# ScalarE casts the second block's weights before the operands of the sums; 13 temporaries in a norm; pools laid out anew

## The chip, the cores and the metric

The kernel runs on one core of one Trainium2 chip. The metric is the device time of one launch in microseconds (us); of the kernel before, three runs are known. One launch was also recorded by the hardware profiler; all rows below come from that record. The core's engines are TensorE (PE, matrix products), VectorE (DVE), ScalarE (ACT), GpSimd (POOL) and SyncE (SP, which here only starts transfers).

## The reference

The reference is a trunk of two layers on 1024 prompt tokens and 64 sample tokens, 1088 columns in all. Each layer has a mixer (layer 0: attention and a gated recurrence; layer 1, "odd": a convolution and a linear recurrence) and a feed-forward part. Cut to what matters here:

```python
for l in range(2):
    hn = rms_norm(x, norm_mix[l]) * (1 + sc1) + sh1
    o = even_mix(hn, ...) if l == 0 else odd_mix(hn, ...)
    x = x + (1 + g1) * o
    hn = rms_norm(x, norm_ffn[l]) * (1 + sc2) + sh2
    x = x + (1 + g2) * ((silu(hn @ wg[l]) * (hn @ wu[l])) @ wd[l])
y = rms_norm(x, final_norm)
```

D_MODEL is 1024, the hidden width of the feed-forward part is 2816. Everything is float32.

## The kernel before, in words

Tokens lie along the free dimension, features along the 128 partitions; x is 8 tiles of 128x1088. Each float32 operand of a product is split into a high part (a cast on ACT, `split`, shown as L99) and a low part (operand minus high part, on POOL or DVE, L100), and each product is three products: high by high, high by low and low by high.

The program runs in stages: mix (layer 0, to about 878 us), up half of layer 0 (to about 1380), down half of layer 0 (`ffn0`, to about 1697; its last part also works out the norm statistics and the first projections of the next mixer), odd (to about 2059), up half of layer 1 (to about 2525), down half of layer 1.

**The up half.** It makes 22 blocks of 128 hidden rows, f = 0 to 21, from weights wg and wu. Block 0 is computed while the normalised input is made (its last matmuls are `ps_z`; L385 is ACT's silu of the gate, L386 DVE's multiplication by the up part, L397 the transfer of the finished hidden block). Block 1 (`plain_block`, matmuls at L381) uses the plain input operands and four half weights: wg and wu give two halves each, each half cast on ACT (`wh`) and subtracted on POOL (`wl`). Blocks 2 to 21 (matmuls at L509, in the changed kernel L507) use a scheme with seven products instead of eight, X, Y, Z, W, X, Z, W, whose operands are sums of quarters of the input. `sums()` makes those operands once per layer: ACT adds the shift into x in place (L472, 16 instructions: a 1024- and a 64-column part of each of 8 tiles), DVE subtracts quarters (L477 to L480, 16 instructions of 128x544), and 16 quarters are split, by a cast on ACT and a subtraction on DVE (L99 and L100, `op`). Each block's weights are combined too: `weights(f)` yields the first half weight as it is fetched (X), and the second (Y) after three additions on DVE (s1, wu, wg: these carry L51).

Two `cbc` tiles are also made in the up half: a sigmoid on ACT (L186) and a product on DVE (L187), for the modulation vectors of later stages; the sigmoid and the silu need different ACT tables, so an ACT_TABLE_LOAD stands wherever they follow each other.

**What sets the order.** Instructions made through `oS`, `oV`, `oPE` (class InOrder, so the line shown is L51) keep the order of the source among themselves; the others are placed by the scheduler from their priorities (`soon()` raises them, `later()` lowers them). Each engine then runs its own list strictly in order and waits at an instruction until what it reads is there. `layout` places the buffers of a stage's pool by tag; a tile waits for the last users of the old tile at its address.

**The norm in ffn0's tail.** The squares of the 8 x tiles (`ntmp`) are summed for one chunk of columns after the other; ACT makes some of the squares (L256, L260; for the last chunk L51), DVE adds them (L261, L263), PE reduces them over the partitions (`ps_o <- ones, ntmp`), POOL takes the power (L234, `r`), and then x is normalised (L273, L279, L276, L277).

**The odd stage** handles one of 8 column groups j after the other: each iteration has two projections whose weights are loaded by `load_x` and `load_g`, a convolution (`xc`), gates (`rg`, `mu`), a scan and a part of the output.

Of the kernel before, what the change touches and what calls it, by code (L numbers as in the profile page):

```python
# [10 lines left out]
F32 = mybir.dt.float32  # L11
# [3 lines left out]
AF = mybir.ActivationFunctionType  # L15
ALU = mybir.AluOpType

P = 128
# [36 lines left out]
def hybrid_encoder(ctx: ExitStack, tc: tile.TileContext, I, O):  # L55
# [369 lines left out]
    def up_half(l, plain, x, t_tag, op_tag, ada):  # L425
        B = B12, B11, B21, B22 = plain[0]
        with phase_pool(f"up{l}") as fp:
            layout(fp, ("t4", NT, 4), ("t1", NT, 4), ("t3", NT, 4), ("pad", 72, 1), ("wg", 1024, 2), ("wu", 1024, 1),
                   ("wh", 512, 5), ("cbc", 1024, 2), ("s1", 512, 1), ("wl", 512, 5), ("hid0", NT, 2))
# [6 lines left out]
            def w_split(src, pair=None):  # L436
                hi, lo = pair or w_pair()
                with soon():
                    split(src, hi, lo, G)
                return hi, lo  # L440
# [26 lines left out]
            def sums():  # L467

                for k in range(KD):
                    for r0, rn, b in rng(0, NT):  # L470
                        v = x[k][:, r0:r0 + rn]
                        S.activation(v, v, AF.Identity, bias=mods[l][:, 3 * KD + k, b:b + 1])  # L472
                T1, T3, T4 = ([halves(fp.tile([P, NT], F32R, name="op", tag=t, bufs=4)) for _ in range(4)]
                              for t in ("t1", "t3", "t4"))
                for k in range(4):
                    a, b, c, d = x[k][:, :HT], x[k][:, HT:], x[k + 4][:, :HT], x[k + 4][:, HT:]
                    V.tensor_sub(d, b, d)  # L477
                    V.tensor_sub(b, b, a)
                    V.tensor_sub(a, a, d)
                    V.tensor_sub(c, c, a)  # L480
                    split(d, T3[k][:, 0, :], T3[k][:, 1, :], V)
                    split(b, T1[k][:, 0, :], T1[k][:, 1, :], V)
                    split(c, T4[k][:, 0, :], T4[k][:, 1, :], V)
                T2 = []
                for k in range(4):
                    T2.append(halves(u(op_tag, F32R, "op")))
                    split(x[k][:, :HT], T2[k][:, 0, :], T2[k][:, 1, :], V)
                return B11, T2, T3, T1, B21, T4, B22

            stage["open"].close()  # L490
            with psum_pool(f"acc{l}", *(("acc" + n, 1024, 1) for n in "XYZW")):
# [3 lines left out]
                def plain_block(f, order):  # L495
                    hid = hid0()
                    pairs = [w_pair() for _ in range(4)]
                    ws = [w_split(w, pairs[(i + 1) % 4]) for i, w in enumerate(fetch(f))]
                    for n, ci in zip("XYZW", order):
                        acc = new_acc(n)  # L500
                        plain_chunk(ci, ws, B, hid, acc[:, 0, :Q], acc[:, 1, :Q], PE)
                    dma(hid_dram[f], hid)
# [9 lines left out]

                ops = sums()
                plain_block(1, (1, 3, 0, 2))
# [109 lines left out]
    with phase_pool("mix") as mp:  # L624
        stage["w"] = mp
        layout(mp, ("w_hi", 1024, 2), ("w_lo", 1024, 2), ("be", 1152, 6), ("om", 1024, 2), ("w_raw", 1024, 2),
               ("sm", 512, 3), ("qs", 512, 2), ("junk", 512, 1), ("wt", 1152, 2), ("kv", 1664, 3))
# [571 lines left out]
    with phase_pool("ffn0") as fp:  # L1199
        stage["w"] = fp  # L1200
        layout(fp, ("hid", 2 * NT, 2), ("ntmp", 384, 8), ("wd_lo", 1024, 6), ("wd_hi", 1024, 6), ("w_raw", 1024, 2))
        ntmp = lambda: fp.tile([P, 384], F32, name="ntmp", tag="ntmp", bufs=8)
# [48 lines left out]
    with phase_pool("odd") as gp:  # L1251
        w2 = stage["w"] = gp
        layout(gp, ("un", 1094, 10), ("wx_raw", 1024, 1), ("gw", 256, 1), ("gwh", 256, 1), ("gwl", 256, 1),
               ("pad", 840, 1), ("wd_hi", 1024, 2), ("wd_lo", 1024, 2), ("w_hi", 1024, 2), ("w_raw", 1024, 2),
               ("w_lo", 1024, 2))
# [5 lines left out]
        def load_x(j, S=oS):  # L1261
            return load_w(wio[8 + j], S=S)

        def load_g(j, S=oS):
            return load_w(wio[j], S=S)
# [90 lines left out]
        wx_, wg_ = (load_w(wio[i], w2, "wd", lo_eng=V) for i in (9, 1))  # L1356
# [242 lines left out]
```

## Time and profile before

| | |
|---|---|
| median of 3 runs | 2816.09 us |
| lowest and highest | 2810.23 and 2822.07 us |
| the profiled execution itself | 2812.69 us |
| its span in the trace | 2810.9 us |
| mean granted TensorE clock | 0.96 |
| PE / PE's weight loads | 2625.3 us (93%) / 2564.3 us (91%) |
| DVE | 1846.9 us (66%) |
| ACT | 1017.7 us (36%) |
| POOL | 1179.5 us (42%) |

A row of the timeline gives start, duration, engine, line, operation, output and inputs, the count of like instructions in a row, and in brackets how long the engine had been idle before it and what released it. Matmul ends are modelled and overlap the next start a little. The granted clock is a share of 2.4 GHz: 0.50 is 1.2 GHz.

### The profile page before, as it was taken

What the parts mean: (1) busy time and instruction counts of PE and PEld (TensorE: products, weight loads), DVE (VectorE), ACT (ScalarE), POOL (GpSimd) and SP (SyncE); (2) the same over time, 40 slices, a digit from 0 to 9 for tenths busy, and PEclk for the clock granted to TensorE, in tenths of its full rate; (3) what the DMA queues carried; (4) which work ended last, traced back from release to release, by engine and by line L of the source; (5) the groups of instructions that cost most, each with busy time, mean ns of one, the idle gap of its engine ahead of it and who ended that gap; (6) DMA issues with size and microseconds to landing.
All of it is one profiled execution on the core that took longest, in us unless ns stands there. A gap on an engine that the chain in (4) does not pass through costs nothing. (4 is left out here: it accounts for less than half of the span.)

```text
span 2810.9 us, 44600 instructions
## 1 busy us (share of the span) xinstructions
PE 2625.3 (93%) x17680; PEld 2564.3 (91%) x17680; DVE 1846.9 (66%) x2850; ACT 1017.7 (36%) x1858; POOL 1179.5 (42%) x795
## 2 busy tenths in 40 slices
PE   6999999999987899999999978998979999999998
PEld 6898989998877899999999978998879999999997
DVE  8768763667898578876465575658867444446556
ACT  3225343354456333333221145563453222223112
POOL 6445443455440577765322223444126444433112
PEclk9899989899999899999999989999989999999999
DMA  6232111113113244443332101121313222226211
GB/s 240 90 108 90 47 62 55 58 55 126 58 48 110 95 141 136 130 136 109 150 130 93 62 25 57 66 72 58 109 49 126 78 78 85 69 84 224 88 64 64
DMA packets 99664, 261.98 MB, mean 93 GB/s; under 512 B 16641, under 2 KB 36097, under 8 KB 99457
## 3 DMA queue, kind: packets, MB, share of 16 engines
q1 hardware_dynamic: 99168, 258.03, 27.6%
q8 instruction: 139, 2.28, 0.3%
q10 hardware_dynamic: 288, 1.11, 0.1%
q14 instruction: 69, 0.56, 0.1%
HBM read 208.41 MB, written 50.69 MB: 92 GB/s over the span
## 5 line engine op out<-in xcount | busy, mean ns | idle before, releaser
L100 POOL TENSOR_TENSOR w_lo<-w_raw,w_hi 128x1024 fp32r<-128x1024 f32 x92 | 236.7, 2579 | 536.2 <-ACT w_hi L99 481.3
L100 POOL TENSOR_TENSOR wl<-wg,wh 128x512 fp32r<-128x512 f32 x164 | 231.1, 1415 | 381.0 <-ACT wh L99 371.4
L509 PE MATMUL accZ<-op,wh 128*128 128x272 f32 x1280 | 244.8, 289 | 5.6 <-DVE tmp L51 5.6
L509 PE MATMUL accW<-op,wh 128*128 128x272 f32 x1280 | 243.6, 288 | 0.0
L509 PE MATMUL accX<-op,wh 128*128 128x272 f32 x1280 | 243.6, 288 | 0.0
L99 ACT CAST w_hi<-w_raw 128x1024 fp32r<-128x1024 f32 x90 | 93.2, 1050 | 361.0 <-PE ps_mm L313 251.7
L129 PE MATMUL ps_mm<-h_hi,w_hi 128*128 128x384 f32 (+1 forms) x624 | 213.1, 342 | 2.3 <-ACT w_hi L99 1.1
L129 PE MATMUL ps_mm<-h_hi,w_lo 128*128 128x384 f32 (+1 forms) x624 | 212.2, 341 | 1.9 <-POOL w_lo L100 1.9
L129 PE MATMUL ps_mm<-h_lo,w_hi 128*128 128x384 f32 (+1 forms) x624 | 211.8, 339 | 0.0
L509 PEld LDWEIGHTS accZ<-op,wh 128*128 128x128 f32 x1280 | 200.7, 188 | 7.4 <-DVE tmp L51 6.0
L99 ACT CAST wh<-wg 128x512 fp32r<-128x512 f32 x164 | 99.9, 619 | 288.9 <-DVE wg L51 167.5
L318 DVE SCALAR_TENSOR_TENSOR x<-ps_mm,mods,x 128x384 f32<-128x384 f32 (+4 forms) x334 | 151.9, 479 | 75.0 <-PE ps_mm L313 74.0
L509 PEld LDWEIGHTS accX<-op,wh 128*128 128x128 f32 x1280 | 201.0, 188 | 0.0
L509 PEld LDWEIGHTS accW<-op,wh 128*128 128x128 f32 x1280 | 200.9, 188 | 0.0
L509 PE MATMUL accZ<-op,wl 128*128 128x272 f32 x640 | 184.6, 288 | 1.0 <-POOL wl L100 1.0
L509 PE MATMUL accX<-op,wl 128*128 128x272 f32 x640 | 184.5, 288 | 0.0
L509 PE MATMUL accW<-op,wl 128*128 128x272 f32 x640 | 184.5, 288 | 0.0
L318 DVE SCALAR_TENSOR_TENSOR x<-ps_t,mods,x 128x384 f32<-128x384 f32 (+3 forms) x220 | 107.0, 503 | 88.3 <-PE ps_t L313 88.2
L51 DVE SCALAR_TENSOR_TENSOR tmp<-hid,cbc 128x1024 f32<-128x1024 f32 x68 | 131.0, 1927 | 21.6 <-ACT tmp L194 20.9
L100 POOL TENSOR_TENSOR wl<-wu,wh 128x512 fp32r<-128x512 f32 x84 | 129.2, 1539 | 31.8 <-ACT wh L99 31.3
L318 DVE SCALAR_TENSOR_TENSOR x<-ps_z,mods,x 128x384 f32<-128x384 f32 (+2 forms) x198 | 91.4, 484 | 61.6 <-PE ps_z L313 61.0
L51 DVE TENSOR_TENSOR tmp<-tmp 128x544 f32<-128x544 f32 x80 | 106.8, 1335 | 32.8 <-ACT tmp L563 29.4
(482 smaller groups left out, 8083.2 us busy)
## 6 DMA issues: line engine op xcount, KB each, us to landing
hid<-in_adaT SPq DMA_DIRECT2D x48, 512.0 KB, 4.0
w_raw<-in_wd SPq DMA_DIRECT2D x44, 512.0 KB, 4.1
hid_dram<-tmp SPq DMA_DIRECT2D x80, 272.0 KB, 2.1
hid_lo<-hid_dram SPq DMA_DIRECT2D x40, 544.0 KB, 5.2
wg<-in_wg SPq DMA_DIRECT2D x42, 512.0 KB, 3.9
wu<-in_wu SPq DMA_DIRECT2D x42, 512.0 KB, 3.6
w_raw<-in_w_in_even SPq DMA_DIRECT2D x28, 512.0 KB, 3.8
w_raw<-in_adaT SPq DMA_DIRECT2D x24, 512.0 KB, 3.7
```

Of the source, the lines that this page charges most:

```text
L51: return lambda *a, **k: self.tc.keep_in_program_order(f(*a, **k))
L99: S.copy(hi, src)
L100: (lo_eng or G).tensor_sub(lo, src, hi.bitcast(F32))
L129: PE.matmul(ps[:, :n], a[:, k * P:(k + 1) * P], b[:, c0:c0 + n], start=(i == 0), stop=(i == last))
L318: V.scalar_tensor_tensor(x[m][:, r0:r0 + rn], ps[:, r0 - c0:r0 - c0 + rn], gate[:, m, b:b + 1], x[m][:, r0:r0 + rn], ALU.mult, ALU.add)
L509: PE.matmul(acc[:, j, :Q], a[:, k * P:(k + 1) * P], op[k][:, b, c], start=(start == 1 and i == 0), stop=(i == 11), skip_group_check=True)
```

## The change

The diff has five pieces:

1. In `up_half`, the fetch and the split of block 1's weights move from `plain_block` to before `sums()`, and their casts keep the order of the source (`oS`). In `sums()` the 16 L472 instructions and the casts of the T1, T3 and T4 operands do so too; the T2 casts don't.
2. The layouts of the stages up, mix and odd list their tags in another order (some pads differ).
3. In `ffn0`, `ntmp` has 13 buffers instead of 8.
4. In odd, the loads of odd j use the buffers "w", those of even j "wd" (before: always "w").
5. The first two loads of odd use "w" (before "wd").

```diff
     def up_half(l, plain, x, t_tag, op_tag, ada):
...
-            layout(fp, ("t4", NT, 4), ("t1", NT, 4), ("t3", NT, 4), ("pad", 72, 1), ("wg", 1024, 2), ("wu", 1024, 1),
-                   ("wh", 512, 5), ("cbc", 1024, 2), ("s1", 512, 1), ("wl", 512, 5), ("hid0", NT, 2))
+            layout(fp, ("t4", NT, 4), ("t1", NT, 4), ("t3", NT, 4), ("pad", 72, 1), ("wg", 1024, 2), ("wl", 512, 5),
+                   ("cbc", 1024, 2), ("hid0", NT, 2), ("s1", 512, 1), ("wh", 512, 5), ("wu", 1024, 1))
...
-            def w_split(src, pair=None):
+            def w_split(src, pair=None, S=S):
                 hi, lo = pair or w_pair()
                 with soon():
-                    split(src, hi, lo, G)
+                    split(src, hi, lo, G, S=S)
                 return hi, lo
...
-                        S.activation(v, v, AF.Identity, bias=mods[l][:, 3 * KD + k, b:b + 1])
+                        oS.activation(v, v, AF.Identity, bias=mods[l][:, 3 * KD + k, b:b + 1])
...
-                    split(d, T3[k][:, 0, :], T3[k][:, 1, :], V)
-                    split(b, T1[k][:, 0, :], T1[k][:, 1, :], V)
-                    split(c, T4[k][:, 0, :], T4[k][:, 1, :], V)
+                    split(d, T3[k][:, 0, :], T3[k][:, 1, :], V, S=oS)
+                    split(b, T1[k][:, 0, :], T1[k][:, 1, :], V, S=oS)
+                    split(c, T4[k][:, 0, :], T4[k][:, 1, :], V, S=oS)
...
-                def plain_block(f, order):
+                def plain_block(f, order, ws):
                     hid = hid0()
-                    pairs = [w_pair() for _ in range(4)]
-                    ws = [w_split(w, pairs[(i + 1) % 4]) for i, w in enumerate(fetch(f))]
...
+                pairs = [w_pair() for _ in range(4)]
+                ws = [w_split(w, pairs[(i + 1) % 4], oS) for i, w in enumerate(fetch(1))]
                 ops = sums()
-                plain_block(1, (1, 3, 0, 2))
+                plain_block(1, (1, 3, 0, 2), ws)
...
-        layout(fp, ("hid", 2 * NT, 2), ("ntmp", 384, 8), ("wd_lo", 1024, 6), ("wd_hi", 1024, 6), ("w_raw", 1024, 2))
-        ntmp = lambda: fp.tile([P, 384], F32, name="ntmp", tag="ntmp", bufs=8)
+        layout(fp, ("hid", 2 * NT, 2), ("ntmp", 384, 13), ("wd_lo", 1024, 6), ("wd_hi", 1024, 6), ("w_raw", 1024, 2))
+        ntmp = lambda: fp.tile([P, 384], F32, name="ntmp", tag="ntmp", bufs=13)
...
         def load_x(j, S=oS):
-            return load_w(wio[8 + j], S=S)
+            return load_w(wio[8 + j], None, "w" if j % 2 else "wd", S=S)
 
         def load_g(j, S=oS):
-            return load_w(wio[j], S=S)
+            return load_w(wio[j], None, "w" if j % 2 else "wd", S=S)
...
-        wx_, wg_ = (load_w(wio[i], w2, "wd", lo_eng=V) for i in (9, 1))
+        wx_, wg_ = (load_w(wio[i], lo_eng=V) for i in (9, 1))
```

**ACT at the end of block 0, layer 0.** `hid_8165` is block 0's hidden block. The list before:

```order
L472 ACTIVATE x<-x,mods_69 128x64
L385 ACTIVATE hid_8165<-ps_z 128x272
L397 DMA hid_dram_89<-hid_8165 128x1088
L99 CAST op<-x 128x544 x12
L99 CAST wh<-wg 128x512 x2
L99 CAST wh<-wu 128x512 x2
L99 CAST wh<-wg 128x512
L385 ACTIVATE hid_8620<-accX 128x272
```

And now:

```order
L364 ACTIVATE op<-x,mods_69 128x64
L385 ACTIVATE hid_8165<-ps_z 128x272
L397 DMA hid_dram_89<-hid_8165 128x1088
L51 CAST wh<-wg 128x512 x2
L51 CAST wh<-wu 128x512 x2
L51 ACTIVATE x<-x,mods_69 128x1024
L51 ACTIVATE x<-x,mods_69 128x64
```

The four casts of block 1's weights have moved ahead of the twelve operand casts. The 16 activations on x, which stood before block 0's last silu, now all stand behind the weight casts; only the first pair is shown.

**ACT further on, from the fourth chunk of block 1 to the first weights of block 2.** `accX` in the COPY is block 2's first product; the wg cast behind it is block 2's second weight (Y). Before:

```order
L385 ACTIVATE hid_8620<-accZ 128x272
L99 CAST wh<-wg 128x512
L99 CAST wh<-wu 128x512
L99 CAST wh<-s_8871 128x512
L99 CAST wh<-wg 128x512
L385 ACTIVATE hid_8620<-accW 128x272
L99 CAST wh<-wu 128x512
L535 COPY tmp<-accX 128x544
```

Now:

```order
L385 ACTIVATE hid_8640<-accZ 128x272
L99 CAST op<-x 128x544 x2
L385 ACTIVATE hid_8640<-accW 128x272
L51 CAST op<-x 128x544 x3
L535 COPY tmp<-accX 128x544
L51 CAST op<-x 128x544
L99 CAST wh<-wg 128x512
L99 CAST wh<-wu 128x512
```

The casts of block 2's combined weights stood ahead of the silu of accW; now six operand casts, that silu and the COPY of the finished product X of block 2 stand ahead of them.

**DVE in the same place.** The last row of each is the addition that makes block 2's Y weight. Before:

```order
L100 TENSOR_TENSOR op<-x,op 128x544 x12
L386 TENSOR_TENSOR hid_8620<-hid_8620,accX 128x272
L187 TENSOR_TENSOR cbc<-cbc,hid_8856 128x1024
L100 TENSOR_TENSOR op<-x,op 128x544 x3
L187 TENSOR_TENSOR cbc<-cbc,hid_8856 128x1024
L51 TENSOR_TENSOR s_8871<-wu 128x512
L100 TENSOR_TENSOR op<-x,op 128x544
L386 TENSOR_TENSOR hid_8620<-hid_8620,accY 128x272
L51 TENSOR_TENSOR wu<-wg,wu 128x512
L51 TENSOR_TENSOR wg<-s_8871,wg 128x512
```

Now:

```order
L187 TENSOR_TENSOR cbc<-cbc,hid_8856 128x1024
L51 TENSOR_TENSOR s_8871<-wu 128x512
L386 TENSOR_TENSOR hid_8640<-hid_8640,accZ 128x272
L100 TENSOR_TENSOR op<-x,op 128x544
L480 TENSOR_TENSOR x<-x 128x544
L100 TENSOR_TENSOR op<-x,op 128x544
L386 TENSOR_TENSOR hid_8640<-hid_8640,accW 128x272
L100 TENSOR_TENSOR op<-x,op 128x544 x2
L51 TENSOR_TENSOR wu<-wg,wu 128x512
L100 TENSOR_TENSOR op<-x,op 128x544 x2
L51 TENSOR_TENSOR wg<-s_8871,wg 128x512
```

Two of the multiplications for block 1 (accZ, accW) stood behind the addition and now stand ahead of it, and the subtractions for the operands are spread up to it. The last of the L100 pair reads the operand that ACT casts behind its COPY. Layer 1 has the same order in all three places.

## Rows read from the trace of the kernel before

**Rows 1.** The page, part 1: busy us, share of the span, instructions.
```profile
PE 2625.3 (93%) x17680; PEld 2564.3 (91%) x17680; DVE 1846.9 (66%) x2850; ACT 1017.7 (36%) x1858; POOL 1179.5 (42%) x795
```

**Rows 2.** Waits of PE: what it waited for, us in total, times, longest.
```profile
PE accX L381 <- ACT wh L99: 17.3, 1, 17.3
...
PE ps_t L51 <- ACT xh L51: 5.4, 1, 5.4
```

**Rows 3.** Timeline of PE, layer 0, blocks 1 (L381) and 2 (L509).
```profile
917.98 0.82 PE L381 MATMUL accX<-op,wh 128*128 128x272 f32 x2 [12.64 <-DVE op L100]
...
923.58 0.60 PE L381 MATMUL accX<-op,wl 128*128 128x272 f32 x1 [3.42 <-POOL wl L100]
...
952.39 0.41 PE L509 MATMUL accY<-op,wh 128*128 128x272 f32 x2
```

**Rows 4.** Timeline of ACT in the same stretch.
```profile
898.56 9.30 ACT L472 ACTIVATE x<-x,mods 128x64 f32<-128x64 f32 x15
...
910.75 6.66 ACT L99 CAST op<-x 128x544 fp32r<-128x544 f32 x12 [2.61 <-DVE hid L386]
917.32 1.13 ACT L99 CAST wh<-wg 128x512 fp32r<-128x512 f32 x2
...
933.70 1.28 ACT L186 ACT_TABLE_LOAD   x1
934.99 1.06 ACT L186 ACTIVATE hid<-cbc 128x1024 f32<-128x1024 f32 x1
```

**Rows 5.** Timeline of DVE in the same stretch.
```profile
909.90 0.43 DVE L386 TENSOR_TENSOR hid<-hid,ps_z 128x272 f32<-128x272 f32 x1
...
914.70 7.70 DVE L100 TENSOR_TENSOR op<-x,op 128x544 fp32r<-128x544 f32 x12
...
936.09 1.22 DVE L187 TENSOR_TENSOR cbc<-cbc,hid 128x1024 f32<-128x1024 f32 x1 [1.94 <-ACT hid L186]
...
942.64 0.69 DVE L51 TENSOR_TENSOR wg<-s,wg 128x512 f32<-128x512 f32 x1
```

**Rows 6.** Timeline of POOL in the same stretch.
```profile
918.00 6.75 POOL L100 TENSOR_TENSOR wl<-wg,wh 128x512 fp32r<-128x512 f32 x2 [27.16 <-ACT wh L99]
924.72 2.50 POOL L100 TENSOR_TENSOR wl<-wu,wh 128x512 fp32r<-128x512 f32 x2
```

**Rows 7.** Timeline of PE, layer 1: block 1, and Y of block 2.
```profile
2075.93 0.82 PE L381 MATMUL accX<-op,wh 128*128 128x272 f32 x2 [17.26 <-ACT wh L99]
...
2105.03 0.41 PE L509 MATMUL accY<-op,wh 128*128 128x272 f32 x2
```

**Rows 8.** Start of layer 0's down half: PE's timeline.
```profile
1384.76 0.69 PE L313 MATMUL ps_t<-hid_hi,w_hi 128*128 128x384 f32 x1 [4.85 <-ACT w_hi L99]
```

**Rows 9.** Windows there: us; PE, PEld, DVE, ACT, POOL busy; granted clock, DMA share, GB/s.
```profile
1384.00:1390.00 6.00, 5.24 (x16) 5.25 (x17) 0.00 (x0) 1.75 (x2) 4.69 (x2) 0.50 1.00 357
```

**Rows 10.** Tail of ffn0, norm of the next layer: timelines of ACT.
```profile
1664.74 1.12 ACT L279 ACTIVATE ntmp<-ntmp,mods 128x384 f32<-128x384 f32 x2 [8.22 <-DVE ntmp L273]
...
1673.07 1.18 ACT L51 ACTIVATE ntmp<-x 128x320 f32<-128x320 f32 x3
```

**Rows 11.** The same place: timeline of PE.
```profile
1676.66 1.41 PE L51 MATMUL ps_o<-ones,ntmp 128*128 128x1 f32 x6 [12.66 <-DVE ntmp L263]
```

**Rows 12.** Odd, j = 0 to 2: timeline of POOL.
```profile
1714.96 2.54 POOL L1308 TENSOR_TENSOR rg<-rg,xc 128x1088 f32<-128x1088 f32 x1 [13.01 <-ACT rg L51]
1719.44 2.64 POOL L100 TENSOR_TENSOR w_lo<-wx_raw,w_hi 128x1024 fp32r<-128x1024 f32 x1 [1.94 <-ACT w_hi L99]
...
1749.75 2.53 POOL L1308 TENSOR_TENSOR rg<-rg,xc 128x1088 f32<-128x1088 f32 x1 [13.10 <-ACT rg L51]
...
1778.15 2.55 POOL L1308 TENSOR_TENSOR rg<-rg,xc 128x1088 f32<-128x1088 f32 x1 [7.33 <-ACT rg L51]
```

**Rows 13.** The same stretch: timeline of DVE.
```profile
1719.94 3.30 DVE L51 SCALAR_TENSOR_TENSOR mu<-rg,mu 128x1088 f32<-128x1088 f32 x1
...
1754.63 1.29 DVE L51 SCALAR_TENSOR_TENSOR mu<-rg,mu 128x1088 f32<-128x1088 f32 x1
```

More of the change, by code (lines that the diff above doesn't have):

```diff
@@ L626, in hybrid_encoder @@
         layout(mp, ("w_hi", 1024, 2), ("w_lo", 1024, 2), ("be", 1152, 6), ("om", 1024, 2), ("w_raw", 1024, 2),
-               ("sm", 512, 3), ("qs", 512, 2), ("junk", 512, 1), ("wt", 1152, 2), ("kv", 1664, 3))
+               ("qs", 512, 2), ("sm", 512, 3), ("kv", 1664, 3), ("junk", 512, 1), ("wt", 1152, 2))
         masks = mp.tile([P, 6, P], U8, name="masks")
@@ L1253, in hybrid_encoder @@
         layout(gp, ("un", 1094, 10), ("wx_raw", 1024, 1), ("gw", 256, 1), ("gwh", 256, 1), ("gwl", 256, 1),
-               ("pad", 840, 1), ("wd_hi", 1024, 2), ("wd_lo", 1024, 2), ("w_hi", 1024, 2), ("w_raw", 1024, 2),
-               ("w_lo", 1024, 2))
+               ("wd_hi", 1024, 2), ("pad", 700, 1), ("w_hi", 1024, 2), ("w_lo", 1024, 2), ("wd_lo", 1024, 2),
+               ("w_raw", 1024, 2))
         un_ = lambda name, dt=F32, w=NT: gp.tile([P, w], dt, name=name, tag="un", bufs=10)
```

## The prediction

> **What bounds the kernel now.** I read the page's shares first: PE is busy for 2625.3 of 2810.9 us [rows 1], so a change gains only where PE stands still. The second view is the table of PE's waits: the longest single wait, 17.3 us at L381 for a weight cast, and one of 5.4 us in the odd stage [rows 2]. Third come the timelines around L381. In layer 0 PE starts block 1 at 917.98 after 12.64 us of idle, so block 0 ended at 905.34 (my t0); it waits 3.42 us more for the first low weight, and block 2's Y begins at 952.39 [rows 3], which is t0 + 47.05. In layer 1 t0 is 2075.93 - 17.26 = 2058.67 and Y begins at 2105.03, t0 + 46.36 [rows 7]. The reason stands on ACT: twelve operand casts (6.66 us) run ahead of the first weight cast at 917.32 [rows 4]. The bracket of rows 3 names DVE; the cast was equally late. So the two starts are bound by ACT's order, and I follow the changed order on each engine until PE again runs as in the trace before, which is from Y on.
>
> **Up half, block 1.** After t0, DVE's last multiplication takes 0.43 us, and from its end to ACT's next cast pass 0.42 us (910.33 to 910.75), in which ACT starts the transfer [rows 4, 5]. Two weight casts take 1.13 us [rows 4], some 0.6 for the first. So the first weight is ready at about 905.34 + 0.43 + 0.42 + 0.6 = 906.8, the fourth at 908.35; PE stands for 1.5 us instead of 12.64. POOL subtracts a weight in 2.50 / 2 = 1.25 us [rows 6] and DVE is idle then, so the first low weight is there at 908.1, not 923.58. From that point to Y the trace has 952.39 - 923.58 = 28.8 us, the rest of block 1 and product X [rows 3]. X would thus end at 936.9. If Y could begin there, the layer would gain 15.5 us.
>
> **Up half, the sums.** It can't. The 16 activations on x now start only at 908.35; they take 9.30 / 15 = 0.62 us each [rows 4]. DVE's first subtraction reads tiles 0 and 4, ten activations: 908.35 + 6.3 = 914.65, where before it was under way at t0. Up to the addition that makes Y's weight, DVE's list holds 16 subtractions and 16 L100 at 7.70 / 12 = 0.64 (20.5 us), four L386 at 0.43 (1.7), two L187 at 1.22 (2.4) and three additions at 0.69 (2.1) [rows 5], together 26.7, less about 0.7 for the overlap of neighbours: 26. One POOL subtraction (X's low weight) falls among them. In odd the same pair of engines shows what that can cost: a DVE instruction of 1.29 us took 3.30 beside a POOL subtraction that had begun 0.50 us earlier and ran until 1722.08 [rows 12, 13]. I charge 0.9 us, the 1.25 less the 0.35 of an L386 that may lie beside it; the bounds are 0 and 1.25. So the weight is added at 914.65 + 26.9 = 941.55, cast at 942.15 and its low part is there at 943.4. PE does six of the matmuls (Y, Z, W, 0.75 us at full clock) meanwhile, so Y effectively begins at 942.65, t0 + 37.3. PE stands still from 936.9 to 942.15: a new wait of 5.3 us. How early block 1 starts no longer decides; DVE's list does.
>
> Gains: layer 0, 47.05 - 37.3 = 9.75; layer 1, by the same order, 46.36 - 37.3 = 9.05. A stall of this size lowers the clock: after an idle of 4.85 us at 1384.76 the granted clock was 0.50, that is 1.2 GHz, up to 1390 [rows 8, 9], 5.2 us at half speed, worth 2.6. Part of that passes while PE waits for the low weight, so I take 2.2 per layer (bounds 0 and 2.6). The low clock at block 1 costs nothing extra, as block 1 has 5.3 us to spare. Net 7.5 and 6.8.
>
> Two waits on other engines lie under this. ACT's casts and silus share the 26 us with DVE: 16 casts at 0.55 (8.9), four table loads at 1.28 (5.1), two sigmoids at 1.06 (2.1) [rows 4], four silus and the COPY (some 2.2), 18.3 in all: shorter than DVE's 26. And the COPY of X now stands ahead of the last operand's cast, so Y can never follow X directly: COPY 0.6, cast 0.55, L100 0.64, addition 0.69, cast 0.6 make at least 3.1 us. Behind the COPY on ACT are the six weight casts of block 2.
>
> The change adds two table loads to ACT per layer. The trace has 1.28 us for one [rows 4]. The Trainium skill (ScalarE: Activation LUTs, section What ACT_TABLE_LOAD costs) gives about 2.7 us with the drain. By that figure four loads would take 5.7 us more than in my sum, ACT would pass DVE and each layer would gain about 4 us less; the row decides.
>
> **Norm in ffn0's tail.** PE waits 12.66 us until 1676.66 for the last sum of squares [rows 11]. ACT's last squares end at 1674.25, though it was idle for 8.22 us before 1664.74 [rows 10]. With 13 buffers, four squares of the last chunk (0.4 us each) go into that idle time, so the last square ends about 1.9 us earlier, and DVE, which needed 2.2 us behind the last, about 1.0. That is 3.2 less; squares that now precede the normalising of the first chunk cost 0.8. I take 2.4 (bounds 4 and 0; the rows show no buffer wait of its own).
>
> **Odd.** From j = 0 to 1 the iteration took 1749.75 - 1714.96 = 34.8 us, the next one 28.4 [rows 12]. The excess of 6.4 contains the wait of 5.4 [rows 2], and in it stand two POOL subtractions of `wx_raw` (one is shown), beside which DVE is slowed [rows 12, 13]. The buffers' new turn moves these two to j = 5 to 6, to the same places in the iteration. I take 0; bounds -6.4 (nobody waits there) and +6.4 (paid there, and something else at j = 0). The layouts add waits on old tiles, all on users that are several us older in the trace: 0, with the same 6.4 as bound upward for the lot.
>
> **Sum.** 7.5 + 6.8 + 2.4 = 16.7 us off 2812.69, the profiled execution's own time (its span is 1.8 shorter): 2796.0, -0.59%. The median of the runs lies 3.4 above that execution: 2816.1 - 16.7 = 2799.4, so I predict 2799.
>
> **Rivals.**
> 1. *DVE's list is covered better.* If block 1 and X are the limit, Y comes at the 3.1 us floor, 936.9 + 3.1 + 0.5 for the low weight, with no loss of clock: gains 11.9 and 11.2, and the norm 3.2, -26; if the odd wait also vanishes, -33. Time 2783 to 2790. It needs DVE's list 2.1 us shorter than I sum it. For it: 0.9 is there if POOL doesn't block, and the new stand of 1.5 us at block 1 may leave the clock up. Against: the 26 us count from ACT's tenth activation, and PE can't shorten them.
> 2. *POOL is shut out.* Beside DVE's twelve L100, POOL's two subtractions took 6.75 us instead of 2.50, and DVE kept 0.64 [rows 5, 6]. If X's low weight gets through only when DVE first has to wait, near the end of its list (about 939), X runs from 940.2 to 943, and the floor puts Y at 946.9: gains 5.5 and 4.8, less 2.2 each, plus 2.4: -8, 2808. Against: DVE waits for ACT's silus and sigmoids earlier, and POOL has 16 us to find a gap.
> The Trainium skill (SBUF — State Buffer, section SBUF: two separate sides) says that GpSimd and a DVE instruction with two SBUF inputs share a port pair that whichever starts first holds for its whole instruction, while the other stands. Both places agree: POOL stood behind DVE here, DVE behind POOL in odd.
> 3. *Slower: ACT and DVE take turns.* Every operand goes from DVE to ACT and back. If ACT's 18.3 us lay wholly between DVE's 26 instead of beside them, Y would come at t0 + 55.6: losses of 8.6 and 9.3, 2.2 each for the clock, less 2.4: +20, 2836. It decides from 7.5 us per layer on; half of 18.3 would eat the gain. Against: before, casts at 0.55 and L100 at 0.64 ran beside each other without a gap [rows 4, 5].
>
> **Chances.** The forecast 0.57, with its own range 2793 to 2806; rival 1 0.15, rival 2 0.20, rival 3 0.08. Differences under 0.5%, 14 us, can't be told from no change. Of the forecast's share about 0.42 lies beyond that, since its bounds (clock, POOL, norm, odd) reach down to 10 us. Faster: 0.42 + 0.15 = 0.57; same: 0.15 + 0.20 = 0.35; slower 0.08. The range is 2785 to 2812, from rival 1 to rival 2.
>
> **What would show it.** Right: PE idle 1.5 us ahead of L381 in both layers, then 4 to 6 us ahead of Y, released by ACT's wh cast, with the clock at 0.50 behind it; the last sum of squares some 3 us earlier after the same work; the `wx_raw` subtractions at j = 5 to 6 with an iteration near 35 us there. Wrong: a wait for POOL's wl inside X (rival 2), a wait ahead of Y above 13 us (rival 3) or near 3 us (rival 1), or a second long iteration in odd.

## The result, and the profile after

Over seven runs of each kernel, the changed kernel takes 2799.53 us (median; 2790.15 to 2801.73) and the kernel before 2813.62 us (2809.46 to 2822.07). The measured ratio is 0.9942, with a 95% interval of 0.9925 to 0.996: between 11 and 21 us faster (the two medians alone lie 14.1 us apart). The forecast was 2799. All rows below without another name are from one profiled execution of the changed kernel, with a span of 2800.0 us against 2810.9 before.

Shares first, as in [rows 1] (busy us, share of the span, instructions):

```profile
PE 2616.5 (93%) x17680; PEld 2553.8 (91%) x17680; DVE 1855.6 (66%) x2850; ACT 1022.0 (36%) x1862; POOL 1180.6 (42%) x795
```

The waits of PE (us in total, times, longest) answer to [rows 2]:

```profile
PE accY L507 <- ACT wh L99: 16.1, 3, 8.0
...
PE ps_o L51 <- DVE ntmp L263: 13.3, 2, 12.6
...
PE ps_t L51 <- ACT xh L51: 6.8, 7, 4.9
...
PE accX L381 <- ACT wh L51: 3.3, 2, 1.7
```

The waits of 17.3 and 12.6 us at L381 have become two of 1.7. In their place stand two of 8.0 us ahead of block 2's Y (L507; L509 before). The wait in odd for `xh` is still there, 4.9 instead of 5.4, and the norm's last sum waits 12.6 as it did.

PE in layer 0, as in [rows 3] (start, duration, what, and in brackets the idle time before it with its releaser); the last row is the first of the down half:

```profile
908.88 0.52 PE L381 MATMUL accX<-op,wh 128*128 128x272 f32 x2 [1.69 <-ACT wh L51]
...
936.42 0.29 PE L507 MATMUL accX<-op,wl 128*128 128x272 f32 x1
944.66 0.82 PE L507 MATMUL accY<-op,wh 128*128 128x272 f32 x2 [7.95 <-ACT wh L99]
...
1378.89 0.69 PE L313 MATMUL ps_t<-hid_hi,w_hi 128*128 128x384 f32 x1 [4.60 <-ACT w_hi L99]
```

Block 0 ends at 908.88 - 1.69 = 907.19 (t0), and PE runs out of work ahead of the down half at 1378.89 - 4.60 = 1374.29. I call the difference, 467.10 us, the up half's length; before it was 1379.91 - 905.34 = 474.57 [rows 3, 8]. Layer 1, as in [rows 7]:

```profile
2055.91 0.51 PE L381 MATMUL accX<-op,wh 128*128 128x272 f32 x2 [1.62 <-ACT wh L51]
...
2091.68 0.82 PE L507 MATMUL accY<-op,wh 128*128 128x272 f32 x2 [7.95 <-ACT wh L99]
...
2519.28 0.69 PE L313 MATMUL ps_t<-hid_hi,w_hi 128*128 128x384 f32 x1 [5.26 <-ACT w_hi L99]
```

Its length is 2514.02 - 2054.29 = 459.73. Before, the last of these rows read

```profile
2530.24 0.69 PE L313 MATMUL ps_t<-hid_hi,w_hi 128*128 128x384 f32 x1 [4.97 <-ACT w_hi L99]
```

so it was 2525.27 - 2058.67 = 466.60. The 10.9 us between the two profiled executions, stage by stage:

| stretch | before | after | difference |
|---|---|---|---|
| start to t0 of layer 0 | 905.34 | 907.19 | +1.85 |
| up half, layer 0 | 474.57 | 467.10 | -7.5 |
| down half to the last sum of squares | 296.75 | 296.26 | -0.5 |
| from there to the `rg` product of j = 0 in odd | 38.30 | 38.45 | +0.15 |
| odd, j = 0 to 6 | 177.50 | 177.19 | -0.3 |
| odd, j = 6 to t0 of layer 1 | 166.21 | 168.10 | +1.9 |
| up half, layer 1 | 466.60 | 459.73 | -6.9 |
| down half to the end | 285.63 | 285.98 | +0.35 |

Only the two up halves are findings here. The first line can't be laid to the change: e7 and e11 below are one kernel, and its two profiled executions reached t0 at 899.19 and 902.93 us; over all the profiled executions below t0 lies between 893.1 and 907.2. Other stretches move too in kernels that have the same code there: the one up to the last sum of squares takes 295.97 to 299.29 us in the seven kernels with the changed norm, the last one 285.20 to 288.96. So one execution's span can't settle a difference of 10 us; lengths counted from t0 can, and I use those.

What sets Y's start can be read from three engines. ACT, as in [rows 4]:

```profile
908.21 1.14 ACT L51 CAST wh<-wg 128x512 fp32r<-128x512 f32 x2 [3.57 <-DVE hid L386]
...
910.30 8.83 ACT L51 ACTIVATE x<-x,mods 128x1024 f32<-128x1024 f32 x13
...
943.99 0.62 ACT L99 CAST wh<-wg 128x512 fp32r<-128x512 f32 x1 [4.08 <-DVE wg L51]
```

DVE, as in [rows 5]:

```profile
916.83 0.72 DVE L477 TENSOR_TENSOR x<-x 128x544 f32<-128x544 f32 x1 [9.09 <-ACT x L51]
...
920.14 1.82 DVE L480 TENSOR_TENSOR x<-x 128x544 f32<-128x544 f32 x1
...
943.28 0.68 DVE L51 TENSOR_TENSOR wg<-s,wg 128x512 f32<-128x512 f32 x1
```

POOL, as in [rows 6]:

```profile
908.91 2.54 POOL L100 TENSOR_TENSOR wl<-wg,wh 128x512 fp32r<-128x512 f32 x2 [16.20 <-ACT wh L51]
...
919.72 1.67 POOL L100 TENSOR_TENSOR wl<-wg,wh 128x512 fp32r<-128x512 f32 x1 [5.76 <-ACT wh L99]
```

ACT waits 4.08 us for DVE's addition at 943.28, casts, and PE starts. DVE has had no gap since 916.83, when the first subtraction's inputs were shifted. POOL's subtractions ran undisturbed at 908.91, since DVE was idle; the later one met one DVE instruction, which took 1.82 instead of 0.64. That DVE's list sets Y's start, and not PE's progress, shows in five kernels that share this list (the changed kernel, e1, e6, e7 and e11 below), in both layers of each: Y starts 27.82 to 27.84 us after DVE's first subtraction, while product X ends anywhere from 29.4 to 34.6 us after t0. e7 and e11, one kernel profiled twice, show it alone: X ended at t0 + 29.5 and t0 + 31.0 in layer 0, Y began at t0 + 37.49 and t0 + 37.45. The row of e11, whose t0 is 902.93:

```profile
940.38 0.82 PE L514 MATMUL accY<-op,wh 128*128 128x272 f32 x2 [6.42 <-ACT wh L99]
```

The clock, as in [rows 9]:

```profile
909.00:939.00 30.00, 27.61 (x216) 27.18 (x216) 22.13 (x33) 29.46 (x46) 6.62 (x5) 1.00 0.22 73
...
944.00:947.00 3.00, 2.34 (x9) 2.22 (x10) 2.96 (x3) 2.68 (x5) 2.32 (x2) 0.50 0.47 165
947.00:952.00 5.00, 5.00 (x35) 5.00 (x35) 1.35 (x3) 0.00 (x0) 5.00 (x4) 0.83 0.39 108
```

Behind the stall it is 0.50, that is 1.2 GHz. From 944.66 on PE loses 2.34 x 0.5 + 5 x 0.17 = 2.0 us by that.

### The profile page after: what moved, and what is told of

The parts are those of the page before. It is cut to its first block, busy times and chain, and to the rows that moved or that the text cites. A ratio compares the mean times of both kernels' runs of the same rounds, so it can differ in the third digit from the quotient of the medians.

```text
span 2800.0 us, 44597 instructions
## 1 busy us (share of the span) xinstructions
PE 2616.5 (93%) x17680; PEld 2553.8 (91%) x17680; DVE 1855.6 (66%) x2850; ACT 1022.0 (36%) x1862; POOL 1180.6 (42%) x795
## 5 line engine op out<-in xcount | busy, mean ns | idle before, releaser
L100 POOL TENSOR_TENSOR w_lo<-w_raw,w_hi 128x1024 fp32r<-128x1024 f32 x92 | 237.3, 2586 | 533.9 <-ACT w_hi L99 484.6
L100 POOL TENSOR_TENSOR wl<-wg,wh 128x512 fp32r<-128x512 f32 x164 | 225.4, 1381 | 375.6 <-ACT wh L99 333.6
L507 PE MATMUL accZ<-op,wh 128*128 128x272 f32 x1280 | 245.5, 289 | 5.8 <-DVE tmp L51 5.7
L507 PE MATMUL accW<-op,wh 128*128 128x272 f32 x1280 | 244.3, 288 | 0.0
L507 PE MATMUL accX<-op,wh 128*128 128x272 f32 x1280 | 243.5, 288 | 0.0
L507 PEld LDWEIGHTS accZ<-op,wh 128*128 128x128 f32 x1280 | 201.1, 188 | 7.6 <-DVE tmp L51 6.2
L507 PEld LDWEIGHTS accW<-op,wh 128*128 128x128 f32 x1280 | 201.3, 188 | 0.0
L507 PEld LDWEIGHTS accX<-op,wh 128*128 128x128 f32 x1280 | 200.9, 188 | 0.0
L507 PE MATMUL accZ<-op,wl 128*128 128x272 f32 x640 | 184.6, 288 | 1.0 <-POOL wl L100 1.0
L507 PE MATMUL accX<-op,wl 128*128 128x272 f32 x640 | 184.5, 288 | 0.0
L507 PE MATMUL accW<-op,wl 128*128 128x272 f32 x640 | 184.5, 288 | 0.0
L318 DVE SCALAR_TENSOR_TENSOR x<-ps_t,mods,x 128x384 f32<-128x384 f32 (+3 forms) x220 | 107.1, 504 | 87.9 <-PE ps_t L313 87.9
L100 POOL TENSOR_TENSOR wl<-wu,wh 128x512 fp32r<-128x512 f32 x84 | 131.7, 1569 | 27.9 <-ACT wh L99 27.3
L507 PE MATMUL accY<-op,wh 128*128 128x272 f32 x640 | 124.7, 292 | 16.1 <-ACT wh L99 16.1
```

Source lines behind the costliest of these rows:

```text
L100: (lo_eng or G).tensor_sub(lo, src, hi.bitcast(F32))
L318: V.scalar_tensor_tensor(x[m][:, r0:r0 + rn], ps[:, r0 - c0:r0 - c0 + rn], gate[:, m, b:b + 1], x[m][:, r0:r0 + rn], ALU.mult, ALU.add)
L507: PE.matmul(acc[:, j, :Q], a[:, k * P:(k + 1) * P], op[k][:, b, c], start=(start == 1 and i == 0), stop=(i == 11), skip_group_check=True)
```

## The experiments

Lengths and waits are from each kernel's profiled execution, in us; the ratio is to the kernel before, timed on the same chip, with its 95% interval. "First Z wait" is the moment, counted from t0 of layer 0, at which PE ends its wait of about 0.65 us ahead of block 5's first accZ for DVE's `tmp`; every kernel has this wait.

| kernel | ratio | layer 0 | layer 1 | ahead of block 1 / its low weight / Y or Y's low weight, layer 0 | first Z wait |
|---|---|---|---|---|---|
| before | | 474.57 | 466.60 | 12.64 / 3.42 / - | 111.6 |
| changed | 0.9942 [0.9925, 0.996] | 467.10 | 459.73 | 1.69 / - / 7.95 | 104.1 |
| e1_up_alone | 0.9962 [0.995, 0.9974] | 470.73 | 462.07 | 4.42 / - / 6.99 | 107.1 |
| e2_rest_alone | 1.0004 [0.9994, 1.0013] | 475.13 | 468.65 | 12.63 / 3.42 / - | 111.5 |
| e3_early_adds | 0.9938 [0.9923, 0.9953] | 467.70 | 461.51 | 1.69 / - / 1.21 | 104.1 |
| e4_shift_first | 0.998 [0.997, 0.999] | 471.64 | 466.88 | 11.85 / - / 0.83 | 108.6 |
| e5_shift_early | 0.9983 [0.9972, 0.9994] | 474.55 | 461.39 | 6.02 / 9.98 / - | 111.7 |
| e6_old_mix_layout | one run, 2797.17 | 470.45 | 459.75 | 4.72 / - / 5.90 | 106.9 |
| e7_pool_later | one run, 2793.38 | 467.27 | 459.65 | 1.69 / - / 7.97 | 104.1 |
| e8_both | 0.9979 [0.9968, 0.999] | 474.92 | 461.08 | 6.11 / 9.98 / - | 111.5 |
| e9_dve_splits | 0.9936 [0.9924, 0.9949] | 465.56 | 461.59 | 6.06 / 1.83 / - | 102.5 |
| e10_dve_first_norm | 0.9934 [0.9918, 0.9949] | 465.48 | 460.15 | 5.37 / 2.42 / - | 102.4 |
| e11_norm_edit | 0.9942 [0.993, 0.9954] | 468.49 | 459.87 | 1.68 / - / 6.42 | 103.8 |

In every row layer 0's length less the first Z wait is between 362.8 and 364.7, so the layer is decided in its first 110 us. e7 and e11 are one kernel profiled twice: their lengths differ by 1.2 and 0.2 us, and less than that is no finding.

### Which piece: e1 and e2

e1 is the kernel before with the up half's piece alone (its layout too); e2 is the changed kernel without it. The middle of e1's edit:

```diff
...
-                ops = sums()
-                plain_block(1, (1, 3, 0, 2))
+                pairs = [w_pair() for _ in range(4)]
+                ws = [w_split(w, pairs[(i + 1) % 4], oS) for i, w in enumerate(fetch(1))]
+                ops = sums()
+                plain_block(1, (1, 3, 0, 2), ws)
...
```

> The kernel before with the change in the up halves alone (casts of block 1's weights first, program order kept, the up layout). Theory A (the gain lies in the two starts of the up halves, and DVE's list sets where product Y begins): 14 us faster than before (ratio 0.995); PE waits 1.6 us at L381 and 8.0 us at Y in both layers; the odd stage keeps its long iteration of 34.8 us at j = 0 to 1. Rival B (the gain comes from the norm, odd or the layouts): within 4 us of before.

> The changed kernel with the change in the up halves undone: 13 temporaries, the odd buffers and the mix and odd layouts alone. Theory A: 0 to 2 us slower than before; the waits at L381 stay at 12.6 + 3.4 and 17.3 us, the wait for the last sum of squares at 12.6, and the long odd iteration stands at j = 5 to 6. Rival B: 10 us faster or more.

e2 is the kernel before again, long waits included: the 13 temporaries, the odd buffers and the other layouts bring nothing measurable by themselves. e1 has 8.4 us of the 14.3 by which both lengths fell (by time alone, e1 and the changed kernel can't be told apart). Where the rest went is in ACT's rows of e1, in layers 0 and 1:

```profile
908.34 1.14 ACT L51 CAST wh<-wg 128x512 fp32r<-128x512 f32 x2 [6.30 <-DMA hid_dram<-hid]
...
2060.12 1.14 ACT L51 CAST wh<-wu 128x512 fp32r<-128x512 f32 x2 [1.91 <-DMA wu<-in_wu]
```

The weight casts are first in ACT's list but wait for a transfer: in layer 0 for the one that carries block 0's hidden tile out, in layer 1 for the load of wu, which starts only at 2056.09. DVE's first subtraction then starts 2.7 us (layer 0) and 2.1 us (layer 1) later from t0 than in the changed kernel, and Y the same.

### The layout: e6

The changed kernel with mix's layout of before.

```diff
         layout(mp, ("w_hi", 1024, 2), ("w_lo", 1024, 2), ("be", 1152, 6), ("om", 1024, 2), ("w_raw", 1024, 2),
-               ("qs", 512, 2), ("sm", 512, 3), ("kv", 1664, 3), ("junk", 512, 1), ("wt", 1152, 2))
+               ("sm", 512, 3), ("qs", 512, 2), ("junk", 512, 1), ("wt", 1152, 2), ("kv", 1664, 3))
```

> The changed kernel with the mix layout of before alone. Theory F (block 1's weight tiles in layer 0 then lie over block 0's hidden tile, and their cast waits for that tile's transfer): PE waits 4.4 us at L381 in layer 0 instead of 1.7, and 1.6 in layer 1 as in the changed kernel; the up half of layer 0 takes 3 to 4 us more. Rival: 1.7 in both, the layout of mix changes nothing.

Block 0's hidden tile has the tag kv there. One edit in another stage brings the wait back in layer 0 alone:

```profile
904.32 1.14 ACT L51 CAST wh<-wg 128x512 fp32r<-128x512 f32 x2 [6.60 <-DMA hid_dram<-hid]
```

Layer 0 loses 3.35 us, layer 1 nothing. The order of mix's tags decides whether the weight casts write where block 0's hidden tile lay; if they do, they wait until it has been sent. So mix's layout carries 3.35 us in layer 0 (e6; e1 lacks 3.6). In layer 1 e1 lacks 2.3 us; whether odd's layout or its buffers give them was not separated.

### Take away Y's wait: e3

The three additions for block 2's weights stand ahead of the sums in DVE's list.

```diff
-                yield w_split(w11)
+                first = w_split(w11)
+                if f > 2:
+                    yield first
                 with soon():
                     oV.tensor_add(s1, w21, w22)
                     oV.tensor_add(w21, w11, w21)
                     oV.tensor_add(w11, s1, w11)
+                if f == 2:
+                    yield first
...
+                queue = itertools.chain.from_iterable(weights(f) for f in range(2, FF))
+                ahead = [next(queue)]
                 ops = sums()
...
```

> The changed kernel with the three additions for block 2's weights put ahead of the sums on DVE. Theory A (the wait at Y is DVE's list in front of these additions): the wait of 8.0 us at Y falls below 2 in both layers and the clock stays up; 6 to 9 us per layer, 12 to 18 faster than the changed kernel, 24 to 32 faster than before. Rival C (the wait is ACT's, whose casts and table loads are in the way): the wait stays above 5 us and the time within 4 us of the changed kernel.

The wait of 7.95 us is gone, as theory A has it, but the gain that it forecast isn't there: 467.70 and 461.51, no shorter than in the changed kernel. PE of e3, layer 0:

```profile
894.83 0.52 PE L381 MATMUL accX<-op,wh 128*128 128x272 f32 x2 [1.69 <-ACT wh L51]
...
924.15 0.39 PE L511 MATMUL accY<-op,wl 128*128 128x272 f32 x1 [1.21 <-POOL wl L100]
...
929.89 0.39 PE L511 MATMUL accZ<-op,wh 128*128 128x272 f32 x1 [2.74 <-DVE op L100]
```

With one of 0.58 us that is left out these waits are 4.5 us, and two more of about 1 us follow. DVE in front of the last one:

```profile
924.60 6.95 DVE L100 TENSOR_TENSOR op<-x,op 128x544 fp32r<-128x544 f32 x4
```

and POOL beside it:

```profile
920.50 3.59 POOL L100 TENSOR_TENSOR wl<-wg,wh 128x512 fp32r<-128x512 f32 x1 [19.36 <-ACT wh L99]
924.06 1.77 POOL L100 TENSOR_TENSOR wl<-wu,wh 128x512 fp32r<-128x512 f32 x1
```

Four subtractions that take 0.64 each elsewhere took 6.95. So part of the wait came back at the end of DVE's list. Y starts at t0 + 29.39 in e3, 8.1 us ahead of the changed kernel; at block 3's Y the lead is 3.2 us (t0 + 57.41 against 60.65), at block 4's 2.1 (79.62 against 81.70), at block 5's nothing (102.91 against 102.92). The waits in block 2 and the clock behind them (0.50 from 931 to 934) took the first part, two waits in blocks 3 and 4 that the changed kernel doesn't have most of the rest:

```profile
963.62 0.52 PE L511 MATMUL accZ<-op,wh 128*128 128x272 f32 x2 [0.88 <-DVE tmp L51]
...
986.28 0.52 PE L511 MATMUL accZ<-op,wh 128*128 128x272 f32 x2 [1.10 <-DVE tmp L51]
```

DVE keeps the same time in both kernels there: it adds block 3's accZ to `tmp` at t0 + 69.7 in each (962.84 here, 976.85 in the changed kernel). But it is no longer busy without a gap: at 950.55 it has waited 2.83 us for ACT, and ACT at 957.43 2.23 us for POOL. So behind the sums PE is held by the work on these engines together; which of them sets its pace is not shown. PE at the first Z wait, in the changed kernel and then in e3:

```profile
1011.28 0.49 PE L507 MATMUL accZ<-op,wh 128*128 128x272 f32 x2 [0.65 <-DVE tmp L51]
```

```profile
997.22 0.49 PE L511 MATMUL accZ<-op,wh 128*128 128x272 f32 x2 [0.64 <-DVE tmp L51]
```

From t0 both are 104.1 us away (1011.28 - 907.19 and 997.22 - 893.14). The wait itself says nothing: it has this length in the kernel before too.

### The place of the activations: e4 and e5

In e4 the 16 activations on x stand ahead of the weight casts in the order of the source, in e5 the scheduler places them, which puts them before block 0's last silu as in the kernel before.

```diff
-            def sums():
+            def shift():
                 for k in range(KD):
...
-                        oS.activation(v, v, AF.Identity, bias=mods[l][:, 3 * KD + k, b:b + 1])
+                        S.activation(v, v, AF.Identity, bias=mods[l][:, 3 * KD + k, b:b + 1])
+            def sums():
...
-                pairs = [w_pair() for _ in range(4)]
+                shift(); pairs = [w_pair() for _ in range(4)]
```

(Shown for e5; e4 keeps `oS.activation`.)

> The changed kernel with ACT's 16 activations on x ahead of the casts of block 1's weights, and these ahead of the operand casts. Theory A: PE starts block 1 some 11.6 us after block 0 instead of 1.6, but DVE's list starts 2 us earlier and the addition for Y is made before X ends, so there is no wait at Y: Y begins about 41 us after block 0, against 38 in the changed kernel and 47 before; 3 us per layer slower than the changed kernel, 9 to 12 faster than before. Rival D (what counts is that the weight casts come first of all): no faster than before.

> The changed kernel with ACT's 16 activations on x free to stand ahead of block 0's last silu, as before the change; the casts of block 1's weights still stand ahead of the operand casts. Theory A2 (what binds from t0 on is DVE's whole list of sums, stretched by POOL's subtractions, and not the place of one addition in it: it starts 10 us later in the changed kernel): DVE's first subtraction stands at t0 again, PE restarts 6 us after t0 instead of 1.6, Y follows X with no wait, and an up half takes 3 to 5 us less than in the changed kernel (462 to 464 and 455 to 457 us from t0 to the down half); 6 to 10 us faster than the changed kernel, 22 to 27 faster than before (ratio 0.990 to 0.992). Rival E (the early restart of PE is what counted): an up half takes 4 us more than in the changed kernel, ratio 0.997.

Both fell short. e4 starts Y at t0 + 41.6 with no wait worth naming, as forecast, behind 11.85 us ahead of block 1, the price of the activations; but its layers are 4.5 and 7.2 us longer than the changed kernel's, not 3, and layer 1 is as long as in the kernel before. In e5, where DVE starts 11 us earlier than in the changed kernel counted from t0, I expected the shortest time; PE in layer 0 shows why it isn't so:

```profile
911.48 0.82 PE L381 MATMUL accX<-op,wh 128*128 128x272 f32 x2 [6.02 <-ACT wh L51]
...
923.64 0.60 PE L381 MATMUL accX<-op,wl 128*128 128x272 f32 x1 [9.98 <-POOL wl L100]
```

POOL of e5:

```profile
911.50 13.31 POOL L100 TENSOR_TENSOR wl<-wg,wh 128x512 fp32r<-128x512 f32 x2 [20.53 <-ACT wh L51]
```

DVE of e5 meanwhile:

```profile
914.75 7.71 DVE L100 TENSOR_TENSOR op<-x,op 128x544 fp32r<-128x544 f32 x12
```

Two POOL subtractions (2.54 us in the changed kernel) took 13.31, and end only after DVE's unbroken run, which keeps its 0.64 per instruction. This is the prediction's rival 2, in another kernel than the one it was made for. The Trainium skill (SBUF — State Buffer, section SBUF: two separate sides) has GpSimd and a two-input DVE instruction exclude each other for a whole instruction; that they exclude each other agrees, but one DVE instruction of 0.64 us would account for a delay of 0.64, and the row shows some 11. In layer 1 of e5 the wait for the low weight is 3.01 us, and the length 1.7 above the changed kernel's.

### The low weights on DVE: e9

If POOL's being shut out is the whole trouble of e5, DVE can make block 1's four low weights itself (4 x 0.64 us).

```diff
-            def w_split(src, pair=None, S=S):
+            def w_split(src, pair=None, S=S, lo_eng=G):
...
-                    split(src, hi, lo, G, S=S)
+                    split(src, hi, lo, lo_eng, S=S)
...
-                ws = [w_split(w, pairs[(i + 1) % 4], oS) for i, w in enumerate(fetch(1))]
+                ws = [w_split(w, pairs[(i + 1) % 4], oS, V) for i, w in enumerate(fetch(1))]
```

> The run with the early activations, with the low parts of block 1's four weights subtracted by DVE, ahead of its L100, instead of by POOL. Theory L (POOL was shut out there by DVE's unbroken run of two-input instructions, and this, not the cast, holds PE): PE's wait for block 1's first low weight falls from 10.0 us in layer 0 to 3 or 4 (DVE's subtractions of x still stand ahead), the up half of layer 0 from 474.6 us to 466 to 468; 12 to 18 us faster than before (ratio 0.994 to 0.996). Rival M (POOL was slow for another reason, PE is held by the operands or the clock): the up half of layer 0 stays at 472 to 475 and the time at that of the early activations, 0.998.

PE of e9:

```profile
910.51 0.60 PE L381 MATMUL accX<-op,wl 128*128 128x272 f32 x1 [1.83 <-DVE wl L100]
```

The wait of 9.98 falls to 1.83 and layer 0 from 474.55 to 465.56, as theory L has it (466 to 468), and 1.5 us below the changed kernel's 467.10, little more than one kernel's lengths differ by. In layer 1 the low weight's wait falls too (3.01 to 1.85), but the length stays (461.39, now 461.59).

### The norm: e7, e11

In the changed kernel three of the six POOL subtractions of the chunk before are put behind the last chunk's power.

```diff
         if k not in T2[ci]:
+            if (ci, l, w) == (1, 1, 0) and k in HELD:
+                hi, lo = h[0][k][:, c0:c0 + n], h[1][k][:, c0:c0 + n]
+                S.copy(hi, v)
+                held.append(lambda: oG.tensor_sub(lo, v, hi.bitcast(F32)))
+                return
...
                 rs[ci] = norm_stats(CH[ci], x, ntmp, PE, (), oS if ci == 2 else S)
+                while ci == 2 and held:
+                    held.pop(0)()
```

> The changed kernel with three of POOL's six subtractions for the norm's second chunk put behind the power of the third. Theory G (in the norm DVE stands still beside POOL's subtractions, and that took the gain of the 13 buffers): DVE's last sums take 0.5 us again instead of 1.2, and PE's wait of 12.6 us for the last sum of squares falls by 2 to 2.5. Rival H (DVE waits for ACT's squares): it stays within 0.5 of 12.6.

> The changed kernel with three of POOL's subtractions later in the norm, now timed. Theory G: 2.2 us less than the changed kernel, 18 faster than before, ratio 0.9935 (0.9942 for the changed kernel); the wait for the last sum of squares at 10.4 us as in the first look. Rival: given back behind it, 0.994 or more.

In the changed kernel the squares did move into ACT's idle time, compare [rows 10]:

```profile
1651.26 1.56 ACT L51 ACTIVATE ntmp<-x 128x320 f32<-128x320 f32 x4 [3.36 <-DVE ntmp L261]
...
1665.40 0.47 ACT L51 ACTIVATE ntmp<-x 128x320 f32<-128x320 f32 x1
```

The last square ends at 1665.9, but PE waits as long as in [rows 11]:

```profile
1670.55 1.41 PE L51 MATMUL ps_o<-ones,ntmp 128*128 128x1 f32 x6 [12.62 <-DVE ntmp L263]
```

DVE's additions in between:

```profile
1664.52 1.28 DVE L263 TENSOR_TENSOR ntmp<-ntmp 128x320 f32<-128x320 f32 x1
...
1669.91 0.49 DVE L263 TENSOR_TENSOR ntmp<-ntmp 128x320 f32<-128x320 f32 x1
```

and POOL:

```profile
1663.02 6.11 POOL L100 TENSOR_TENSOR h_lo<-ntmp,h_hi 128x384 fp32r<-128x384 f32 x5 [0.43 <-ACT h_hi L99]
```

While POOL subtracts, an addition takes 1.28 instead of 0.49. In e7, with POOL done earlier, PE's row reads

```profile
1660.57 1.41 PE L51 MATMUL ps_o<-ones,ntmp 128*128 128x1 f32 x6 [10.41 <-DVE ntmp L263]
```

so 2.2 us of the wait are POOL's doing. e11 is the same kernel with five timed runs; its wait is 10.40, but its ratio is the changed kernel's. 2.2 us are 0.08%, less than this measurement resolves. The profiles don't show them given back right behind: from the last sum to odd's first `rg` product it is 38.5 and 38.8 us in e7 and e11, against 38.45 in the changed kernel.

### Both, and a last try: e8, e10

e8 is e5 with e7's edit. e10 is e9 with e7's edit and with one of DVE's subtractions kept in the source's order behind the weights' subtractions:

```diff
-                    V.tensor_sub(d, b, d)
+                    (oV if k == 0 else V).tensor_sub(d, b, d)
```

> Both edits together: the activations on x early, and three of POOL's subtractions later in the norm. Theories A2 and G: 2 us less than the run with the early activations alone, 24 to 29 us faster than before (ratio 0.990). Against them: no faster than the changed kernel (0.994).

> The same with one of DVE's subtractions of x held behind the four weight subtractions, and three of POOL's subtractions later in the norm. Theory L: block 1's first low weight is there 7.6 us after block 0's end, Y follows X without a wait, the up halves take 463 to 466 and 456 to 459 us (changed kernel: 467.1 and 459.7), the norm 2.2 less; 4 to 10 us faster than the changed kernel, ratio 0.990 to 0.9925. Rival N (DVE's list, now 2.5 us longer, holds PE later): no faster than the changed kernel with the norm edit, 0.9935.

e8 inherits e5's wait of 9.98. e10 misses its forecast and hardly differs from e9: PE starts block 1 0.7 us earlier (5.37 against 6.06), the low weight waits 2.42 instead of 1.83, and the lengths 465.48 and 460.15 are those of the changed kernel within 2 us. The intervals of e3, e9, e10, e11 and the changed kernel overlap widely: none of these can be told from it by time.

## Why the prediction was right

**Block 1.** Forecast: idle 1.5 us in both layers. Measured: 1.69 and 1.62. That rests on the layouts, which I costed at nothing: without them it is 4.4 to 4.7 in layer 0 (e1, e6), and layer 1's second pair of casts is late (e1). The sum came out right because I had worked with the new layouts' undisturbed casts without seeing that this was a term, worth some 6 us of the 14.3. That is luck.

**The sums.** Forecast: DVE's list takes 26.9 us from t0 + 9.3 and the addition ends at t0 + 36.2. Measured: it starts at t0 + 9.64 and ends at 943.28 + 0.68, t0 + 36.77, 27.1 us later. The step on the POOL subtraction, 0.9 us, was 1.2 (1.82 against 0.64). Y starts at t0 + 37.47; forecast was 37.3. One sentence beside this sum doesn't come out: 18.3 and 5.7 us of table loads make 24.0 for ACT, under DVE's 26, so "ACT would pass DVE" doesn't follow from it, nor the 4 us.

**The new wait.** Forecast 5.3, measured 7.95 in both layers. X ends at 936.7, t0 + 29.5, not t0 + 31.6, since block 1 ran at clock 1.00 behind a stall of 1.69 us. PE won 2.1 us and waited them off again, as the forecast said it would ("How early block 1 starts no longer decides"); in e11, where block 1 met the lower clock behind 1.68 us, the wait is 6.42 and Y starts at the same distance from t0. The clock's cost of 2.2 was 2.0. Net 7.5 and 6.8 forecast, 7.5 and 6.9 measured.

**Norm.** Forecast 2.4. The wait for the last sum went from 12.66 to 12.62; the stretch up to it is 0.5 us shorter, far less than it moves by itself. The failed step is "the last square ends about 1.9 us earlier, and DVE, which needed 2.2 us behind the last, about 1.0". The squares did end early; DVE did not, because its additions stood beside POOL's subtractions at 1.28 each, and e7 gives 2.2 back by moving three of those. (The sizes were loose too: four squares at 0.4 are 1.6, and 1.9 with 1.2 makes 3.1.) I had read the same slowing in odd [rows 12, 13] and charged it in the up half, but not here.

**Odd.** Forecast 0, with the long iteration moved from j = 0 to j = 5. POOL's rows of the changed kernel:

```profile
1709.00 2.53 POOL L1308 TENSOR_TENSOR rg<-rg,xc 128x1088 f32<-128x1088 f32 x1 [12.35 <-ACT rg L51]
1737.28 2.55 POOL L1308 TENSOR_TENSOR rg<-rg,xc 128x1088 f32<-128x1088 f32 x1 [7.28 <-ACT rg L51]
...
1850.89 2.54 POOL L1308 TENSOR_TENSOR rg<-rg,xc 128x1088 f32<-128x1088 f32 x1 [7.36 <-ACT rg L51]
...
1886.19 2.54 POOL L1308 TENSOR_TENSOR rg<-rg,xc 128x1088 f32<-128x1088 f32 x1
```

28.3 us from j = 0 to 1 (34.8 before) and 35.3 from 5 to 6: right. Behind j = 6 the stretch is 1.9 us longer, most of it in two waits of PE, 6.35 + 1.37:

```profile
1913.77 0.69 PE L313 MATMUL ps_t<-o_hi,w_hi 128*128 128x384 f32 x1 [6.35 <-DVE x L318]
...
1917.42 0.69 PE L313 MATMUL ps_z<-o_hi,w_hi 128*128 128x384 f32 x1 [1.37 <-DVE x L318]
```

where the kernel before has 1.56 + 4.42:

```profile
1915.71 0.44 PE L313 MATMUL ps_t<-o_hi,w_hi 128*128 128x384 f32 x1 [1.56 <-DVE x L318]
...
1921.45 0.69 PE L313 MATMUL ps_z<-o_hi,w_hi 128*128 128x384 f32 x1 [4.42 <-DVE x L318]
```

But the change in odd didn't bring them: e1, which has odd's layout and buffers of before, waits 6.33 and 1.38 there,

```profile
1913.30 0.69 PE L313 MATMUL ps_t<-o_hi,w_hi 128*128 128x384 f32 x1 [6.33 <-DVE x L318]
```

and its stretch is 170.4 us long, against 166.2 in the kernel before and 167.7 to 170.0 in the others. What moves it by 4 us the runs don't show.

**The rivals.** Rival 1, Y at the floor of 3.1 us, fell because DVE's list was as long as summed; e3 adds that an earlier Y alone would not have helped, since its lead of 8.1 us was gone by block 5. Rival 2 is the real danger of this change, but it stood up only where DVE had an unbroken run just as the weights were cast ([rows 5, 6], e5). The changed kernel starts DVE's sums only after 16 activations, and POOL gets its four subtractions in while DVE is idle. e5 shows what it would have cost otherwise: all 7.5 us of layer 0, though only 1.7 us of layer 1. Rival 3 is out: ACT's tables and casts ran beside DVE, which had no gap.

**The time itself.** The forecast of 2799 against 2799.53 is closer than the working deserves. Its base, 2816.1, was the median of three runs and lies 2.5 us above that of seven (2813.62); the norm's 2.4 us, which didn't come, make up for it. What the forecast had right is the 14.3 us of the two up halves, and the new wait in them.

**Open.** Whether any order of ACT and DVE beats these, since three unlike ones (the changed kernel, e3 and e9) have 926.8, 929.2 and 927.2 us for the two lengths together; what holds PE behind the sums in e3; and what moves the stretch behind j = 6 in odd.

## What to carry to other kernels

When a wait of PE goes, sum the list of the engine that feeds it up to the next thing PE needs: PE starts again where that list ends, however early it got going. Moving one item up in the list took that wait away here and brought others, further on, that ate the gain. POOL work that must be ready soon belongs where DVE is idle, even if DVE then starts later. And read what an early instruction writes, too: the address of its output can tie it to a transfer that has nothing to do with it, and a layout change in another stage can take that away.

## What the runs showed of the hardware that was not expected

- A POOL subtraction can be held for the whole of a DVE run, not for one instruction: two took 13.31 us beside DVE's L478 to L480 and L100 (e5, layer 0; 6.84 in its layer 1), and DVE lost nothing in layer 0. In e3 the two took turns instead: four DVE instructions 6.95 us, POOL 1.77 each; in e4 five DVE instructions took 1.80 to 1.82 each beside POOL. What decides between the two was not settled.
- One kernel reached t0 at 899.19 us in one profiled execution (e7) and at 902.93 in another (e11). The granted clock over the 35 us before doesn't order the executions: it was 0.83 in the changed kernel (907.19), and 0.90 in the kernel before (905.34), e11 (902.93) and e3 (893.14).
- The same short idle can lower the granted clock or leave it. Behind 1.69 us it stayed at 1.00 in the changed kernel; behind 1.68 us in e11 it fell, to 0.50 from 907 to 909, and was at 1.00 again from 910. Behind 7.95 us it was 0.50 for some 4 us in the changed kernel.
